# A mixture-of-experts loop: search and gather one rank further ahead, and the turning of a rank's inner layer inside the next rank's first product

## The chip, the cores and the metric

The kernel runs on one core of a Trainium2 chip. The metric is device time in microseconds (us) of one execution. Engines: TensorE (PE; its weight loads are PEld), VectorE (DVE), ScalarE (ACT), GpSimd (POOL), SyncE (SP), which issues loads, and the DMA engines.

## The reference, cut to what matters

One step of a decoder trunk for 520 tokens (512 of a prompt, 8 samples): a combined projection, a state-space branch, dilated attention, two layer norms, and a mixture of 64 experts of which each token takes 8. The change lies in the experts:

```python
for b in blocks:                                  # one expert and the tokens that chose it
    xb = x_pad[tok]                               # gather of its tokens' rows, 1024 wide
    h = jax.nn.silu(xb @ w1[e]) * (xb @ w3[e])    # inner layer, 256 wide
    yb = (h @ w2[e]).astype(jnp.float32)
    acc = acc.at[tok].add(yb * g[:, None])        # scatter, weighted by the gate
```

All in float32. Every expert's weights (w1, w3, w2) are read from HBM once.

## The kernel before

Each float32 operand is split into a high part (ScalarE, L269) and a low part (VectorE, L265; one weight chunk of each expert on GpSimd, L265 too), and a product is three matmuls: high x high, high x low, low x high.

The first 440 us are projection, attention, state space, routing. Then comes the loop over ranks: experts in order of how many tokens they have, most first. `CAPS[e]` (112 down to 56) is the number of rows held for rank e. For a rank e:

- `find(e)`: a small matmul (`x<-what,oh`) looks up the tokens of the rank; VectorE makes their numbers `idx` (L1396). `gather(e)` (L1414, GpSimd) has a DMA fetch their rows to `XG[e % 3]`, one of three buffers, so it waits until rank e-3's rows are turned. `fetch(e)` is both.
- `turn(e)`: eight TensorE transposes of `xg` (L215), in two halves with a PSUM bank each, split into `xgh` and `xgl`.
- `expert_in(e)`: the first product, four weight chunks q0 to q3 of 512 KB, six matmuls each (`a<-hi,xgh`, `a<-lo,xgh`, `a<-hi,xgl`). `ffn_mid` at its end makes `hg` on ScalarE and then VectorE (L259).
- `ffn_turn(e)`: two transposes of `hg` (`a<-ident,hg`), split into `hh` (ScalarE) and `hl` (VectorE). Here it is called H.
- `expert_out(e)`: the second product, chunks k0 and k1, twelve matmuls in six pairs (`mm<-hi,hh`, `mm<-lo,hh`, `mm<-hi,hl`, twice), then `y` (L1450) and a scatter that adds it in HBM (L1451, GpSimd).

Weight chunks are loaded by SyncE in one sequence (L318), in the order q0 to q3 of rank e, then k0 and k1 of rank e-1; raw buffers come free when a chunk is split. Between ranks stands further work of other layers (`x<-ph,x1h` and the like). The transposes of `xg` and `hg` and the first product share three PSUM banks (`bank()`, names `a`).

No order is written out by hand in the loop: a scheduler orders each engine's instructions from the program order, a simulated time line and the constraints given to it (`issue_after`). Each engine then carries out its list in order.

Of the kernel before, what the change touches and what calls it, by code (L numbers as in the profile page):

```python
# [11 lines left out]
def _quiet(*args, **kwargs):  # L12
# [19 lines left out]
NE = 64  # L32
FIXED = 2
CAPS = ([112] * 3 + [100] * 1 + [94] * 1 + [92] * 1 + [88] * 2 + [86] * 1 + [84] * 3 + [82] * 2 + [78] * 7 + [76] * 2 + [74] * 4
        + [72] * 5 + [70] * 4 + [68] * 4 + [66] * 5 + [64] * 7 + [62] * 3 + [60] * 2 + [58] * 2 + [56] * 5)
# [165 lines left out]
def trunk_step(ctx: ExitStack, tc: tile.TileContext, I, O):  # L201
# [3 lines left out]
    class Tensor:  # L205
# [3 lines left out]
        def matmul(self, *a, **k):  # L209
            ins = nc.tensor.matmul(*a, **k)  # L210
            if self.pinned:
                tc.keep_in_program_order(ins)

        def transpose(self, *a, **k):
            ins = nc.tensor.transpose(*a, **k)  # L215
            if self.pinned:
                tc.keep_in_program_order(ins)

    T = Tensor()
# [35 lines left out]
    def bank():  # L255
        return psa.tile([128, 512], F32, tag="a", name="a")
# [10 lines left out]
    def split(hi, lo, src, e=V):  # L267

        a = S.activation(hi, src, AF.Copy)  # L269
        return a, sub(e, lo, src, hi.bitcast(F32))  # L270
# [976 lines left out]
    def ffn_in(out, xth, xtl, hi, lo, q, rows):  # L1247

        for k in range(2):
            kk = 2 * q + k  # L1250
            for n, (l, w) in enumerate(((xth, hi), (xth, lo), (xtl, hi))):
                T.matmul(out, lhsT=l[:, kk, rows], rhs=w[:, k], start=(kk == 0 and n == 0), stop=(kk == 7 and n == 2))

    def ffn_mid(ps, m):
        hg = moe.tile([MAX_CAP, 256], F32, tag="hg", bufs=2, name="hg")
        S.activation(hg[0:m], ps[0:m, 0:256], AF.Silu)
        mul(V, hg[0:m], hg[0:m], ps[0:m, 256:512])
        return hg

    def ffn_turn(hg, m):  # L1260
        ps = bank()
        for k in range(2):
            T.transpose(ps[:, m * k:m * k + m], hg[0:m, 128 * k:128 * k + 128], ident[0:m, 0:m])
        hh, hl = (moe.tile([128, 2, MAX_CAP], F32R, tag=nm, bufs=2, name=nm)[:, :, 0:m] for nm in ("hh", "hl"))
        H['turned'] = split(hh, hl, ps[:, 0:2 * m].rearrange("p (k t) -> p k t", k=2))
        return hh, hl
# [9 lines left out]
    def shared_mid(out, hg):  # L1276
        S.activation(hg, out[:, 0:128], AF.Silu)
        mul(V, hg, hg, out[:, 128:256])
        return hg

    def shared_turn(hg, i, c):

        ps = bank()
        T.transpose(ps[:, 0:TT], hg, ident[0:TT, 0:TT])
        split(H['shared'][:, i, 0, c], H['shared'][:, i, 1, c], ps[:, 0:TT])
# [93 lines left out]
    XG, XT, HG, HT, GC, IX = {}, {}, {}, {}, {}, {}  # L1379
# [3 lines left out]
    def find(e, what=(0, 1)):  # L1383

        m = CAPS[e]
        if e not in OH:
            OH[e] = one_hot(e, m)
        a, b = what[0], what[-1] + 1
        ps = psx.tile([128, 512], F32, tag="x", name="x") if e > 2 else bank()
        for i in R5:  # L1390
            T.matmul(ps[0:m, 3 * a:3 * b], lhsT=OH[e][:, i], rhs=H['what'][:, i, 3 * a:3 * b, e], start=(i == 0), stop=(i == 4))
        both = moe.tile([128, 2], F32, tag="gc", bufs=8, name="both")
        V.tensor_reduce(both[0:m, a:b], ps[0:m, 3 * a:3 * b].rearrange("p (w n) -> p w n", n=3), axis=AX.X, op=ALU.add)
        if 0 in what:
            IX[e] = moe.tile([128, 1], I32, tag="idx", bufs=8, name="idx")
            H['last'] = V.tensor_scalar(IX[e][0:m], both[0:m, 0:1], 1024.0, H['slots'][0:m], op0=ALU.add, op1=ALU.min)  # L1396
        if 1 in what:
            GC[e] = both[:, 1:2]
            if e < NE - 2:
                OH.pop(e)  # L1400
# [7 lines left out]
    def fetch(e):  # L1408
        find(e)
        gather(e)  # L1410

    def gather(e):
        m = CAPS[e]
        G.indirect_dma_start(out=XG[e % 3][0:m], out_offset=None, in_=xD[:, :],  # L1414
                             in_offset=bass.IndirectOffsetOnAxis(ap=IX[e][0:m, 0:1], axis=0),
                             bounds_check=NT - 1, oob_is_err=False)

    def turn(e):
        x, m = XG[e % 3], CAPS[e]
        XT[e] = [moe.tile([128, 8, MAX_CAP], F32R, tag=nm, bufs=2, name=nm)[:, :, 0:m] for nm in ("xgh", "xgl")]  # L1420
        for z in range(2):
            ps = bank()
            for j in range(4):
                k = 4 * z + j
                T.transpose(ps[:, m * j:m * j + m], x[0:m, 128 * k:128 * k + 128], ident[0:m, 0:m])
            src = ps[:, 0:4 * m].rearrange("p (k t) -> p k t", k=4)
            split(XT[e][0][:, 4 * z:4 * z + 4], XT[e][1][:, 4 * z:4 * z + 4], src)

    def expert_in(e):
        ps, m = bank(), CAPS[e]  # L1430
        for q in range(4):
            hi, lo = (t.rearrange("p (k n) -> p k n", k=2) for t in stream.get(AT[e] + q))
            ffn_in(ps[0:m], *XT[e], hi, lo, q, slice(0, m))
        HG[e] = ffn_mid(ps, m)
        XT.pop(e)

# [40 lines left out]
    def second_phase():  # L1477
# [124 lines left out]
        for e in range(NE + 1):  # L1602
            if e == NE - 1:
                last_rows()
            if 0 < e < NE:
                expert_in(e)
            if 0 < e < NE - 1:
                turn(e + 1)
            if e:
                expert_out(e - 1)  # L1610
            else:
                H['shared'] = py.tile([128, 5, 2, 2, TT], F32R, tag="side", name="st")
                mids = py.tile([MAX_CAP, 1024], F32, tag="y", bufs=YB, name="mids")
                mids = [shared_mid(H['first half'][i], mids[0:TT, 128 * i:128 * i + 128]) for i in R5]
            if 0 < e < 6:
                shared_turn(mids[e - 1], e - 1, 0)
            if 0 < e < NE - 1:
                HT[e] = ffn_turn(HG.pop(e), CAPS[e])
            if e + 3 < NE:
                fetch(e + 3)  # L1620
            for i in {SECOND + 2: (0, 1, 2), SECOND + 3: (3, 4)}.get(e, ()):
                second_sums(i)
            if e == 4:
                close_pool(pre)
                pw = open_pool("pw")
            while side and (e - 4) * SIDE >= N_SIDE - len(side) + 1:
                q, i = side.pop(0)
                if q == -2:
                    shared_more(i)
                elif q == -1:  # L1630
                    shared_out(i)
                elif q < 4:
                    layer_inputs(q, i)
                else:
                    last_scales(i)
# [198 lines left out]
    close_pool(gpool)  # L1834
    close_pool(qkv)
    second_phase()


# [16 lines left out]
```

## Time and profile before

| | us |
|---|---|
| median of 3 runs (1320.13 to 1326.46) | 1321.36 |
| profiled execution | 1323.58 |
| its span | 1321.8 |
| TensorE busy | 1182.6 (89%) |
| VectorE busy | 933.0 (71%) |
| ScalarE busy | 702.9 (53%) |
| GpSimd busy | 459.2 (35%) |

HBM moved 234 GB/s over the span; the mean granted TensorE clock was 0.946. Busy times are of the whole span; matmuls overlap, so a busy TensorE needn't be at its peak. Where TensorE isn't the one that is waited for, another engine's idle time costs nothing.

### The profile page before, as it was taken

What the parts mean: (1) busy time and instruction counts of PE and PEld (TensorE: products, weight loads), DVE (VectorE), ACT (ScalarE), POOL (GpSimd) and SP (SyncE); (2) the same over time, 40 slices, a digit from 0 to 9 for tenths busy, and PEclk for the clock granted to TensorE, in tenths of its full rate; (3) what the DMA queues carried; (4) which work ended last, traced back from release to release, by engine and by line L of the source; (5) the groups of instructions that cost most, each with busy time, mean ns of one, the idle gap of its engine ahead of it and who ended that gap; (6) DMA issues with size and microseconds to landing.
All of it is one profiled execution on the core that took longest, in us unless ns stands there. A gap on an engine that the chain in (4) does not pass through costs nothing. (4 is left out here: it accounts for less than half of the span.)

```text
span 1321.8 us, 20417 instructions
## 1 busy us (share of the span) xinstructions
PE 1182.6 (89%) x7082; PEld 884.3 (67%) x7084; DVE 933.0 (71%) x1440; ACT 702.9 (53%) x1055; POOL 459.2 (35%) x285
## 2 busy tenths in 40 slices
PE   6899999999997969888799888899899999988783
PEld 6899899899876846566566566677666666644341
DVE  7965658643487768576779666787878887766566
ACT  3232434233213656566567556677757767666463
POOL 1000000000012346343555335454555455465326
PEclk8899799999998879889999889999999999999897
DMA  9446553252523789889989978999999999979973
GB/s 367 158 135 167 198 162 129 72 155 83 180 77 106 246 217 274 254 263 304 296 254 314 290 237 278 285 329 314 321 311 313 335 314 299 303 249 289 260 230 97
DMA packets 112315, 312.92 MB, mean 237 GB/s; under 512 B 35121, under 2 KB 35545, under 8 KB 111135
## 3 DMA queue, kind: packets, MB, share of 16 engines
q1 hardware_dynamic: 78408, 261.74, 58.8%
q0 software_dynamic: 30848, 43.33, 14.8%
q10 hardware_dynamic: 2953, 6.52, 1.8%
q8 instruction: 57, 0.93, 0.3%
q14 instruction: 49, 0.40, 0.1%
HBM read 276.32 MB, written 32.87 MB: 234 GB/s over the span
## 5 line engine op out<-in xcount | busy, mean ns | idle before, releaser
L265 DVE TENSOR_TENSOR lo<-raw,hi 128x1024 fp32r<-128x1024 f32 x371 | 503.2, 1367 | 203.4 <-ACT hi L269 202.2
L269 ACT ACTIVATE hi<-raw 128x1024 fp32r<-128x1024 f32 x434 | 450.8, 1056 | 279.3 <-DMA raw<-in_we_dram 115.8
L210 PE MATMUL a<-hi,xgh 128*64 128x512 f32 (+18 forms) x512 | 212.3, 415 | 8.5 <-ACT hi L269 6.2
L1451 POOL DMA_INDIRECT accD<-y,idx x62 | 123.2, 1988 | 277.8 <-ACT hh L269 155.6
L210 PE MATMUL a<-lo,xgh 128*64 128x512 f32 (+18 forms) x512 | 210.9, 412 | 6.6 <-DVE lo L265 6.3
L210 PE MATMUL a<-hi,xgl 128*64 128x512 f32 (+18 forms) x512 | 207.0, 404 | 0.0
L265 POOL TENSOR_TENSOR lo<-raw,hi 128x1024 fp32r<-128x1024 f32 x63 | 168.3, 2672 | 62.5 <-ACT hi L269 51.8
L1414 POOL DMA_INDIRECT xg<-xD,idx x64 | 119.0, 1859 | 120.8 <-DVE idx L1396 57.9
L210 PE MATMUL mm<-xh,hi 128*128 128x260 f32 (+2 forms) x576 | 121.3, 292 | 16.6 <-ACT xh L269 6.6
L210 PE MATMUL mm<-xh,lo 128*128 128x260 f32 (+1 forms) x576 | 120.1, 290 | 1.8 <-DVE lo L265 1.8
L210 PE MATMUL mm<-xl,hi 128*128 128x260 f32 (+1 forms) x576 | 120.7, 291 | 0.8 <-DVE xl L265 0.8
L210 PEld LDWEIGHTS a<-hi,xgh 128*64 128x64 f32 (+18 forms) x512 | 75.7, 148 | 53.1 <-ACT hi L269 10.2
L210 PEld LDWEIGHTS a<-lo,xgh 128*64 128x64 f32 (+18 forms) x512 | 75.7, 148 | 45.4 <-DVE lo L265 10.7
L210 PEld LDWEIGHTS mm<-xh,hi 128*128 128x128 f32 x576 | 92.1, 195 | 17.5 <-ACT xh L269 6.3
L210 PEld LDWEIGHTS a<-hi,xgl 128*64 128x64 f32 (+18 forms) x512 | 75.7, 148 | 38.5 <-issue 4.3
L210 PE MATMUL mm<-lo,hh 128*64 128x512 f32 (+18 forms) x256 | 85.5, 416 | 12.8 <-POOL lo L265 9.9
L210 PEld LDWEIGHTS mm<-xh,lo 128*128 128x128 f32 x576 | 92.3, 195 | 2.1 <-DVE lo L265 2.0
L210 PEld LDWEIGHTS mm<-xl,hi 128*128 128x128 f32 x576 | 92.3, 195 | 1.5 <-DVE xl L265 1.1
L210 PE MATMUL mm<-hi,hh 128*64 128x512 f32 (+18 forms) x256 | 85.7, 417 | 8.0 <-ACT hi L269 7.6
L1450 ACT ACTIVATE y<-mm,both 78x1024 f32<-78x1024 f32 (+19 forms) x62 | 68.6, 1106 | 32.9 <-PE mm L210 29.8
L269 ACT ACTIVATE xgh<-a 128x256 fp32r<-128x256 f32 (+17 forms) x128 | 51.0, 408 | 63.7 <-PE a L215 63.0
L215 PEld LDWEIGHTS a<-ident,xg 64*128 64x128 f32 (+18 forms) x512 | 51.1, 147 | 48.9 <-issue 20.0
(410 smaller groups left out, 1919.4 us busy)
## 6 DMA issues: line engine op xcount, KB each, us to landing
raw<-in_we_dram SPq DMA_DIRECT2D x384, 512.0 KB
raw<-in_wd_dram SPq DMA_DIRECT2D x50, 512.0 KB
accD<-zeros_b POOLq DMA_DIRECT2D x2, 2560.0 KB, 23.7
praw<-in_wp_dram SPq DMA_DIRECT2D x8, 512.0 KB
base<-in_xtok_dram ACTq DMA_DIRECT2D x1, 2080.0 KB
xD<-base SPq DMA_DIRECT2D x5, 416.0 KB
base<-accD POOLq DMA_DIRECT2D x5, 416.0 KB, 22.8
acc<-accD SPq DMA_DIRECT2D x5, 416.0 KB
```

Of the source, the lines that this page charges most:

```text
L210: ins = nc.tensor.matmul(*a, **k)
L215: ins = nc.tensor.transpose(*a, **k)
L265: return e.tensor_tensor(out=o, in0=a, in1=b, op=ALU.subtract)
L269: a = S.activation(hi, src, AF.Copy)
L1414: G.indirect_dma_start(out=XG[e % 3][0:m], out_offset=None, in_=xD[:, :], in_offset=bass.IndirectOffsetOnAxis(ap=IX[e][0:m, 0:1], axis=0), ...
L1450: S.activation(y.rearrange("p (h n) -> p h n", h=2), ps[0:m], AF.Copy, scale=GC.pop(e)[0:m])
L1451: G.indirect_dma_start(out=sumsD[e % 2 if e < SECOND else 0][:, :], out_offset=bass.IndirectOffsetOnAxis(ap=IX.pop(e)[0:m, 0:1], axis=0), ...
```

## The change

Two things move. `fetch(e+3)` at the end of an iteration becomes `fetch(e+4)` ahead of `expert_out(e-1)`. And H of rank e-1, which stood behind `expert_out` of the rank before it, is now made inside `expert_in(e)`, held behind the last matmul of its second chunk (`issue_after`). No operation is added or removed.

```diff
@@ -210,6 +210,7 @@
             ins = nc.tensor.matmul(*a, **k)
             if self.pinned:
                 tc.keep_in_program_order(ins)
+            return ins
 
         def transpose(self, *a, **k):
             ins = nc.tensor.transpose(*a, **k)
@@ -1249,7 +1250,8 @@
         for k in range(2):
             kk = 2 * q + k
             for n, (l, w) in enumerate(((xth, hi), (xth, lo), (xtl, hi))):
-                T.matmul(out, lhsT=l[:, kk, rows], rhs=w[:, k], start=(kk == 0 and n == 0), stop=(kk == 7 and n == 2))
+                ins = T.matmul(out, lhsT=l[:, kk, rows], rhs=w[:, k], start=(kk == 0 and n == 0), stop=(kk == 7 and n == 2))
+        return ins
 
     def ffn_mid(ps, m):
         hg = moe.tile([MAX_CAP, 256], F32, tag="hg", bufs=2, name="hg")
@@ -1430,7 +1432,10 @@
         ps, m = bank(), CAPS[e]
         for q in range(4):
             hi, lo = (t.rearrange("p (k n) -> p k n", k=2) for t in stream.get(AT[e] + q))
-            ffn_in(ps[0:m], *XT[e], hi, lo, q, slice(0, m))
+            ins = ffn_in(ps[0:m], *XT[e], hi, lo, q, slice(0, m))
+            if q == 1 and e > 1:
+                with tc.issue_after(ins.ins):
+                    HT[e - 1] = ffn_turn(HG.pop(e - 1), CAPS[e - 1])
         HG[e] = ffn_mid(ps, m)
         XT.pop(e)
 
@@ -1606,6 +1611,8 @@
                 expert_in(e)
             if 0 < e < NE - 1:
                 turn(e + 1)
+            if e and e + 4 < NE:
+                fetch(e + 4)
             if e:
                 expert_out(e - 1)
             else:
@@ -1614,10 +1621,9 @@
                 mids = [shared_mid(H['first half'][i], mids[0:TT, 128 * i:128 * i + 128]) for i in R5]
             if 0 < e < 6:
                 shared_turn(mids[e - 1], e - 1, 0)
-            if 0 < e < NE - 1:
-                HT[e] = ffn_turn(HG.pop(e), CAPS[e])
-            if e + 3 < NE:
-                fetch(e + 3)
+            if e == 0:
+                fetch(3)
+                fetch(4)
             for i in {SECOND + 2: (0, 1, 2), SECOND + 3: (3, 4)}.get(e, ()):
                 second_sums(i)
             if e == 4:
```

What the scheduler makes of it, at three places. GpSimd, around the gather of rank 15 (`xg0`, the first gather row in both pieces); a DMA from `xD` is a gather, one to `accD` a scatter. Before:

```order
L265 TENSOR_TENSOR lo_6134<-raw_5972,hi_6133 128x1024
L1414 DMA xg0_4199<-xD_146,idx_6224 78x1024
L1451 DMA accD1_148<-y_6204,idx_5644 640x1024
L265 TENSOR_TENSOR lo_6287<-raw_6125,hi_6286 128x1024
L1451 DMA accD0_147<-y_6357,idx_5797 640x1024
L265 TENSOR_TENSOR lo_6408<-raw_6278,hi_6407 128x1024
L1414 DMA xg1_4201<-xD_146,idx_6377 78x1024
L1414 DMA xg2_4203<-xD_146,idx_6498 78x1024
```

Now, from the same gather on:

```order
L1416 DMA xg0_4199<-xD_146,idx_6051 78x1024
L1456 DMA accD0_147<-y_6081,idx_5340 640x1024
L266 TENSOR_TENSOR lo_6149<-raw_5980,hi_6148 128x1024
L1416 DMA xg1_4201<-xD_146,idx_6204 78x1024
L1456 DMA accD1_148<-y_6234,idx_5471 640x1024
L266 TENSOR_TENSOR lo_6302<-raw_6133,hi_6301 128x1024
L1416 DMA xg2_4203<-xD_146,idx_6357 78x1024
L1456 DMA accD0_147<-y_6387,idx_5624 640x1024
L266 TENSOR_TENSOR lo_6423<-raw_6286,hi_6422 128x1024
```

The gather of rank 16 (`xg1`) stood behind the scatters of ranks 11 and 12; it now stands behind the scatter of rank 10, ahead of that of rank 11.

TensorE, ranks 5 to 7: `hg_5171` is rank 5's, `a_5244` rank 6's first product, `xg1` rank 7's rows, `mm_5315` rank 5's second product, `hg_5296` rank 6's. Before:

```order
L215 MATMUL a_5222<-ident_69,hg_5171 128x92 x2
L210 MATMUL x_5496<-ph_5365,x1l_3788 104x256
L210 MATMUL a_5244<-hi_5191,xgh_5174 88x512
...
L210 MATMUL a_5244<-hi_5257,xgl_5175 88x512
L215 MATMUL a_5301<-ident_69,xg1_4201 128x88 x4
L215 MATMUL a_5308<-ident_69,xg1_4201 128x88 x4
L210 MATMUL mm_5315<-hi_5269,hh_5225 92x512 x2
L210 MATMUL mm_5315<-lo_5270,hh_5225 92x512 x2
L210 MATMUL mm_5315<-hi_5269,hl_5226 92x512 x2
...
L215 MATMUL a_5343<-ident_69,hg_5296 128x88 x2
L210 MATMUL a_5375<-hi_5316,xgh_5299 88x512
```

Now `hg_5186` is rank 5's, `a_5252` rank 6's first product, `mm_5345` rank 5's second product:

```order
L210 MATMUL a_5252<-hi_5233,xgl_5190 88x512
L216 MATMUL a_5277<-ident_69,hg_5186 128x92 x2
L210 MATMUL a_5252<-hi_5253,xgh_5189 88x512
...
L216 MATMUL a_5316<-ident_69,xg1_4201 128x88 x4
...
L210 MATMUL mm_5345<-hi_5284,hh_5280 92x512 x2
L210 MATMUL mm_5345<-lo_5285,hh_5280 92x512 x2
L216 MATMUL a_5323<-ident_69,xg1_4201 128x88 x4
L210 MATMUL mm_5345<-hi_5284,hl_5281 92x512 x2
L210 MATMUL mm_5345<-hi_5296,hh_5280 92x512 x2
```

H of rank 5 moved from ahead of rank 6's first product to its middle, and H of rank 6 no longer stands between rank 5's second product and rank 7's first. The second half of rank 7's turn moved from ahead of rank 5's second product to between its second and third pair.

VectorE at the same ranks. Before: `lo_5258` is the last chunk of rank 6's first product, `lo_5282` the last of rank 5's second product, `lo_5317` and `lo_5329` the first two of rank 7.

```order
L265 TENSOR_TENSOR lo_5258<-raw_5124,hi_5257 128x1024
L265 TENSOR_TENSOR st_4601<-a_5218,st_4601 128x104
L265 TENSOR_TENSOR hl_5226<-a_5222,hh_5225 128x2x92
L265 TENSOR_TENSOR lo_5282<-raw_5148,hi_5281 128x1024
L265 TENSOR_TENSOR lo_5317<-raw_5163,hi_5316 128x1024
L265 TENSOR_TENSOR lo_5329<-raw_5195,hi_5328 128x1024
L259 TENSOR_TENSOR hg_5296<-hg_5296,a_5244 88x256
L265 TENSOR_TENSOR lo_5377<-raw_5207,hi_5376 128x1024
```

Now `lo_5266` is the last chunk of rank 6's first product, `lo_5297` the last of rank 5's second product, `lo_5347` and `lo_5359` the first two of rank 7:

```order
L266 TENSOR_TENSOR lo_5266<-raw_5132,hi_5265 128x1024
L266 TENSOR_TENSOR st_4601<-a_5248,st_4601 128x104
L266 TENSOR_TENSOR lo_5297<-raw_5163,hi_5296 128x1024
L266 TENSOR_TENSOR lo_5347<-raw_5178,hi_5346 128x1024
L266 TENSOR_TENSOR hl_5281<-a_5277,hh_5280 128x2x92
L266 TENSOR_TENSOR lo_5359<-raw_5225,hi_5358 128x1024
L260 TENSOR_TENSOR hg_5311<-hg_5311,a_5252 88x256
```

`hl` of rank 5 stood behind the last chunk of rank 6's first product; it now stands behind the first chunk of rank 7 as well.

## Rows read from the trace of the kernel before

**Rows 1.** Time by stage: busy PE, PEld, DVE, ACT, POOL, then clock, DMA share, GB/s.

```profile
440.00:883.00 443.00, 385.01 (x2065) 269.30 (x2064) 323.23 (x440) 277.25 (x386) 201.26 (x94) 0.93 0.88 273
883.00:1161.00 278.00, 270.65 (x1562) 179.13 (x1560) 225.53 (x308) 198.64 (x274) 139.17 (x68) 1.00 0.99 314
1161.00:1276.00 115.00, 93.98 (x412) 46.73 (x411) 68.13 (x87) 66.47 (x93) 55.08 (x29) 0.93 0.88 263
```

**Rows 2.** The waits, whole span: us in total, times, longest us.

```profile
ACT hi L269 <- DMA raw<-in_we_dram: 115.8, 83, 3.6
PE a L215 <- DVE hg L259: 23.7, 13, 4.1
PE a L215 <- DMA xg<-xD,idx: 21.5, 5, 10.5
SPq L318 <- DVE lo L265: 328.1, 166, 13.8
```

**Rows 3.** TensorE in order of time, at ranks 4, 16 and 56.

```profile
489.33 1.02 PE L215 MATMUL a<-ident,xg 94*128 94x94 f32 x5 [10.49 <-DMA xg<-xD,idx]
...
659.58 1.30 PE L215 MATMUL a<-ident,xg 78*128 78x78 f32 x8 [5.81 <-DMA xg<-xD,idx]
660.62 1.12 PE L210 MATMUL mm<-lo,hh 128*78 128x512 f32 x2
...
664.94 0.47 PE L215 MATMUL a<-ident,hg 78*128 78x78 f32 x2
...
1171.22 0.68 PE L215 MATMUL a<-ident,xg 60*128 60x60 f32 x4 [4.07 <-DMA xg<-xD,idx]
1171.83 1.11 PE L210 MATMUL mm<-hi,hh 128*62 128x512 f32 x2
```

**Rows 4.** GpSimd in order of time (L1414 gather, L1451 scatter); last row: gathers' landing.

```profile
615.71 1.04 POOL L1414 DMA_INDIRECT xg<-xD,idx  x1 [0.85 <-DVE idx L1396]
623.32 1.49 POOL L1451 DMA_INDIRECT accD<-y,idx  x1 [6.57 <-ACT sg L1277]
...
640.01 1.80 POOL L1414 DMA_INDIRECT xg<-xD,idx  x1 [0.20 <-issue]
...
1140.80 2.55 POOL L265 TENSOR_TENSOR lo<-raw,hi 128x1024 fp32r<-128x1024 f32 x1
...
1154.63 1.23 POOL L1414 DMA_INDIRECT xg<-xD,idx  x1 [0.30 <-issue]
...
DMA to landing us min/median/max: 6.7/13.1/24.4
```

**Rows 5.** TensorE, then VectorE, at the end of rank 5 and start of 7.

```profile
528.41 0.68 PE L210 MATMUL mm<-hi,hh 128*92 128x512 f32 x2
...
529.40 0.62 PE L210 MATMUL mm<-hi,hl 128*92 128x512 f32 x2
...
533.43 0.37 PE L215 MATMUL a<-ident,hg 88*128 88x88 f32 x2 [2.02 <-DVE hg L259]
535.79 0.50 PE L210 MATMUL a<-hi,xgh 128*88 128x512 f32 x1 [1.99 <-DVE xgl L265]
...
530.37 1.23 DVE L265 TENSOR_TENSOR lo<-raw,hi 128x1024 fp32r<-128x1024 f32 x1 [2.32 <-ACT hi L269]
...
532.97 0.41 DVE L259 TENSOR_TENSOR hg<-hg,a 88x256 f32<-88x256 f32 x1
...
535.22 0.95 DVE L265 TENSOR_TENSOR xgl<-a,xgh 128x352 fp32r<-128x352 f32 x2
```

**Rows 6.** VectorE, then TensorE, at ranks 1 and 55 each.

```profile
464.86 4.40 DVE L265 TENSOR_TENSOR lo<-raw,hi 128x1024 fp32r<-128x1024 f32 x2 [0.52 <-ACT hi L269]
...
467.81 0.70 PE L210 MATMUL mm<-hi,hh 128*112 128x512 f32 x2
...
1185.61 1.20 DVE L265 TENSOR_TENSOR lo<-raw,hi 128x1024 fp32r<-128x1024 f32 x1
...
1184.25 0.61 PE L210 MATMUL mm<-hi,hh 128*60 128x512 f32 x2
```

## Prediction

> **What bounds the kernel now.** I began with the time by stage [rows 1]. The expert loop runs from about 440 to 1276 us of a 1321.8 us span. From 440 to 883 us TensorE is busy 385.01 of 443.00 us at a granted clock of 0.93 and the DMA engines are at 0.88 of their share: neither is full. From 883 to 1161 us both are: 270.65 of 278.00 us at 1.00, and 0.99. From 1161 to 1276 us it is 93.98 of 115.00 us, 0.93 and 0.88. So a wait that is taken away can only pay outside the middle stage, and only as far as weights come sooner too.
>
> Then the waits [rows 2]. TensorE waits for `hg` (VectorE's product after the first matmuls of a rank) ahead of the turn of the inner layer, 13 times, 23.7 us in all, 4.1 at most; for a gather 5 times, 21.5 us. ScalarE, which makes the high part of every weight chunk, waits 83 times for the raw weights, 115.8 us, and SyncE's loads wait 166 times (328.1 us, over the whole span) until VectorE's low part has freed a buffer. These two close a loop: loads wait for splits, splits for loads. Whatever makes TensorE faster has to be fed out of that loop.
>
> Last the places. The three large gather stalls are ranks 4, 16 and 56 [rows 3]: 10.49, 5.81 and 4.07 us. After such a stall the matmuls run at the lower clock level for a while: rank 16's five pairs of the second product begin at 660.62 and end where 664.94 begins, 0.86 us a pair [rows 3], where two pairs beside a full clock take 0.99 from 528.41 to 529.40 [rows 5].
>
> **The change, first part: search and gather earlier.** It adds no work: the same 64 searches and gathers are issued, from another place. What matters is where the gather stands in GpSimd's own queue, behind a scatter and a low part or before them. Rank 16 (GpSimd's rows in the change section): its gather was issued at 640.01, behind the scatter of 623.32 and three instructions after it [rows 4], and the rows landed for the matmul at 659.58. In the new order it stands ahead of that scatter. Its buffer is free once rank 13's rows are turned, which was done before the gather of 615.71 [rows 4], so it can go at about 616 to 623: 17 to 24 us earlier than before, where 5.81 were missing. Rank 56: its gather of 1154.63 moves ahead of a scatter to behind the low part of 1140.80 (2.55 us) [rows 4], about 11 us earlier where 4.07 were missing. Both stalls should vanish. A gather takes 13.1 us to land at the median and up to 24.4 [rows 4], so an earlier issue of that size is worth more than the scatter among gathers.
>
> Rank 4 stays: its gather is the same row of GpSimd's list in both kernels; the matmul that waited for it began at 489.33 [rows 3]. A different neighbourhood could change this (rank 5's gather now stands right behind it), so I keep 0 for it, with a bound of 10.49.
>
> Sum of this part: idle 5.81 + 4.07 = 9.88; clock 5 x (0.86 - 0.495) = 1.8 at rank 16, and an estimate of 1.0 at rank 56 from a pair of 1.11 [rows 3] against 0.62 [rows 5]: together 12.7 us. How much of it stays? During a stall raw weights go on arriving until the buffers are full, and the matmuls behind it feed on them. Both places are in stages that are neither TensorE's nor DMA's entirely [rows 1]. With nothing that decides, I take half: -6.4, with bounds of 0 and -12.7.
>
> **Second part: the turn of the inner layer (H) moves from behind the second product of the rank before into the first product of the next rank,** 12 of its 24 matmuls in. TensorE no longer stands still for `hg` there, but it is not free then: the next matmuls need weights and their own turned rows. Ranks 5 and 6 show it [rows 5]. TensorE ends rank 5's second product near 531.4, waits 2.02 us for `hg` (done 533.38), turns, and then waits 1.99 us more for `xgl`, which began on VectorE at 535.22 behind another low part. With the turn moved the first wait disappears and the second one grows by as much: nothing is gained. Where only `hg` was late, it stood behind one low part of 1.23 us [rows 5], and about that much plus `hg`'s own 0.41 is won. If 3 of the 13 places win 1.6 us each, that is 4.9; I take -5, with bounds of 0 and -23.7 [rows 2].
>
> **Third part: what the new order couples.** VectorE carries out its list in order, and the part of the turned inner layer that it makes, `hl`, now stands elsewhere in it. Before, `hl` of rank e stood behind low parts of rank e+1's first product in 61 of 64 ranks, which TensorE needs anyway before it comes to rank e's second product. In the new order it is so in only 33; in 15 it stands behind the low part of the second product's own last chunk, in 16 behind the first chunk of rank e+2 (rank 5 in the change section). The third pair of the second product needs `hl`, and the second half of the next rows' turn takes the PSUM bank that `hl` frees. So in these ranks TensorE waits for a chunk that it wants only later. I priced it from the trace: the end of that low part against the start of the second product plus 0.99 for two pairs. For rank 5: the low part of 530.37 ends 531.60, and `hl` after it was wanted at 528.41 + 0.99 = 529.40 [rows 5]; 2.2 us late. Of ranks 0 to 60, 18 come out late, the first rank 1 by 0.5 (low parts from 464.86 lasting 4.40, product 467.81) and the last rank 55 by 1.6 (1185.61 + 1.20, product 1184.25) [rows 6], 34 us in all.
>
> These 34 us are not 34 us of time. The lateness of neighbours is one and the same lag: weights do not come later for it, and once TensorE runs 2 us behind them the next rank is not late. It also fills idle time that is there: rank 5's 2.2 us fall into the 4.0 us that TensorE then waited anyway [rows 5]. What stays is a small lag in each of the few stretches. I take +4, with bounds of 0 (all of it falls into old idle time) and +34 (all paid).
>
> **Sum.** The profiled execution took 1323.58 us, 2.2 above the median of 1321.36. 1323.6 - 6.4 - 5 + 4 = 1316.2; brought to the median, **1314.0 us**. A measurement of this kernel can tell about 0.5% (6.6 us) from no change, so faster means below 1314.8 and slower above 1328.0.
>
> **The rivals.**
>
> *Weights pace it.* Then TensorE's waits are moved, not removed: with the stalls gone TensorE meets the next chunk sooner and waits for it. For it speak the 0.99 of 883 to 1161 us and the 115.8 us of waits for raw weights [rows 1, 2]; against it the 0.88 in the other two stages, where the stalls are. All of -6.4 and -5 is handed back but 2: about 1319. The Trainium skill ("Perfetto Trace Analysis", Identifying the Most-Contended Engine) says to work on the most contended engine, with HBM utilisation as the measure for DMA; by it this rival would hold for the whole loop, and the trace agrees for the middle stage alone.
>
> *Slower: `hl` behind a later chunk.* If the lag isn't absorbed, because a TensorE that lags frees split buffers later, so that splits, and through them loads, come later too, then half of the 34 us is paid rank after rank, and H wins nothing: +17 - 6.4 = +10.6, about 1332. Slower than 1328.0 begins where some 13 us of the 34 are paid. For it speaks the loop of 328.1 us [rows 2]; against it that ranks 14 to 26 and most of the middle stage are not late.
>
> *More is won.* The gathers' gain stays whole (12.7), H brings 8, the coupling costs 2: -18.7, about 1303. For it speaks that loads wait for splits more than splits for loads [rows 2]. Should rank 4's stall vanish too, it would be up to 10.49 lower still.
>
> *The change doesn't do what it says.* From rank 20 to 39 every gather already stands ahead of the scatter five ranks below it in the old order too; if ranks 16 and 56 stalled for contention and not for their place, nothing is won: 1321 to 1325.
>
> **How the numbers follow.** My forecast (1306 to 1322) has 0.42, two thirds of it below 1314.8; weights pace it 0.19; slower by `hl` 0.22; more is won 0.11; no effect 0.06. Faster: 0.28 + 0.11 + 0.04 (of the weights' case) = 0.43. Slower: 0.22 and 0.03 from the last case's upper end, 0.25. Same: 0.32. The range goes down to 1299 (more is won, with part of rank 4) and up to 1335 (the slower rival at its price and a little more), leaving about 0.08 below and 0.11 above.
>
> **What will show it.** Right, if no wait for a gather stands at ranks 16 and 56 and their gathers are issued some 17 and 11 us earlier; if the row "PE a <- DVE hg" falls from 23.7 to a few us; and if new idle time inside the second product (released by `hl` or by a low part) stays below 10 us. Wrong on the first part, if waits for raw weights or for low parts grow by the 10 us that the gathers free. Wrong on the third, if TensorE's idle time at the third pair or at the turn's second half exceeds 13 us, or if the busy share of 883 to 1161 us falls. The rank 4 stall should still be there with about 10 us; were it gone, the time would be below my forecast for a reason that I left out.

## The result, and the profile after

The changed kernel takes 1333.67 us (median of 5 runs, 1332.94 to 1337.5) where the kernel before, on the same chip, takes 1324.39 (5 runs, 1320.13 to 1326.46): a ratio of 1.0082, interval 1.0053 to 1.0111. It is slower by some 9 to 11 us, where the forecast was 1314.0 against 1321.36, some 7 us faster. The profiled execution took 1332.94 us with a span of 1331.2.

The time by stage of the kernel after, columns as in [rows 1]:

```profile
440.00:883.00 443.00, 370.15 (x1984) 255.44 (x1983) 318.13 (x427) 273.31 (x374) 195.30 (x92) 0.95 0.87 266
883.00:1161.00 278.00, 271.35 (x1586) 181.75 (x1585) 223.46 (x307) 196.69 (x272) 136.74 (x69) 1.00 0.98 314
1161.00:1276.00 115.00, 97.04 (x428) 48.09 (x427) 74.28 (x89) 67.55 (x93) 54.19 (x29) 0.94 0.88 267
```

The loss is in the first of the three stages. There TensorE is busy 370.15 us and carries out 1984 matmuls, where before it was 385.01 us and 2065 [rows 1]. The middle stage is as full as before. DMA isn't fuller in the first stage either: 266 GB/s against 273.

The waits of the kernel after, over the whole span (us in total, times, longest us); first TensorE's, then ScalarE's:

```profile
PE mm L210 <- POOL lo L266: 15.6, 11, 3.3
PE a L216 <- DVE sg L260: 13.8, 5, 5.4
...
PE a L216 <- DVE hl L266: 10.3, 9, 2.9
PE mm L210 <- ACT hh L270: 9.2, 6, 3.3
PE a L216 <- DMA xg<-xD,idx: 8.3, 2, 7.0
...
ACT hi L270 <- DMA raw<-in_we_dram: 147.9, 98, 5.8
```

The two waits that the change was to remove are down. TensorE waits 8.3 us for gathers (21.5 before), and the row "PE a <- DVE hg" of 23.7 us [rows 2] has fallen to 0.7 and is gone from the turn of the inner layer, as the group of that line shows (the number behind the bar's second part is the idle time before it, and what ended it):

```profile
L216 PE MATMUL a<-ident,hg 64*128 64x64 f32 (+17 forms) x128 | 20.3, 239 | 3.7 <-DVE xgl L266 3.7
```

In their place stand a low part that GpSimd makes (15.6), `sg` (13.8), `hl` (10.3) and `hh` (9.2), and ScalarE waits 32 us longer for raw weights than in [rows 2]. `sg` is the inner layer of a further expert that every token goes through; it uses the same two buffers as `hg`. The kernel before has no row of TensorE for `hl`, and for the other three:

```profile
PE mm L210 <- POOL lo L265: 9.9, 11, 1.6
...
PE a L215 <- DVE sg L259: 3.2, 2, 1.8
...
PE mm L210 <- ACT hh L269: 0.4, 1, 0.4
```

TensorE at the three places of [rows 3] in the kernel after, ranks 4, 16 and 56 (start, duration, idle before in brackets), and then the gathers of ranks 16 and 56 on GpSimd, with two rows of rank 16's inputs, the `idx` that its search makes (VectorE) and the end of rank 13's turn (TensorE):

```profile
486.35 0.86 PE L216 MATMUL a<-ident,xg 94*128 94x94 f32 x4 [6.97 <-DMA xg<-xD,idx]
...
663.93 0.43 PE L216 MATMUL a<-ident,xg 78*128 78x78 f32 x4
...
1179.59 0.45 PE L216 MATMUL a<-ident,xg 60*128 60x60 f32 x4
```

```profile
629.94 1.22 POOL L1416 DMA_INDIRECT xg<-xD,idx  x1 [9.46 <-PE mm L210]
632.22 1.51 POOL L1456 DMA_INDIRECT accD<-y,idx  x1 [1.06 <-ACT y L1455]
...
1147.71 1.24 POOL L1416 DMA_INDIRECT xg<-xD,idx  x1 [6.55 <-PE a L216]
...
628.93 0.20 DVE L1398 TENSOR_SCALAR idx<-both,slots 78x1 int32<-78x1 f32 x1
...
628.43 0.45 PE L216 MATMUL a<-ident,xg 82*128 82x82 f32 x4
```

No stall is left at ranks 16 and 56. Their gathers are issued 10.07 and 6.92 us earlier by the clock than in [rows 4], ahead of the scatter, in a loop that runs later by then. That is less than the 17 and 11 us of the forecast. Note the brackets: each gather now stands 6 to 9 us at the head of GpSimd's queue before it can go, with the scatter behind it. Rank 16's `idx` is there at 628.93 + 0.20 = 629.13, and rank 13's rows are turned at 628.43 + 0.45 = 628.88, both within about 1 us of the gather's start at 629.94.

### The profile page after: what moved, and what is told of

It reads as the page before. It is cut to its first block, busy times and chain, and to the rows that moved or that the text cites. A ratio compares the mean times of both kernels' runs of the same rounds, so it can differ in the third digit from the quotient of the medians.

```text
span 1331.2 us, 20434 instructions
## 1 busy us (share of the span) xinstructions
PE 1179.3 (89%) x7083; PEld 878.5 (66%) x7084; DVE 940.5 (71%) x1440; ACT 705.9 (53%) x1055; POOL 455.2 (34%) x285
## 3 DMA queue, kind: packets, MB, share of 16 engines
q0 software_dynamic: 30848, 43.33, 14.8%
## 5 line engine op out<-in xcount | busy, mean ns | idle before, releaser
L266 DVE TENSOR_TENSOR lo<-raw,hi 128x1024 fp32r<-128x1024 f32 x371 | 516.4, 1402 | 219.9 <-ACT hi L270 215.8
L210 PE MATMUL a<-hi,xgh 128*64 128x512 f32 (+18 forms) x512 | 210.0, 410 | 20.7 <-ACT hi L270 12.7
L210 PE MATMUL a<-lo,xgh 128*64 128x512 f32 (+18 forms) x512 | 208.5, 407 | 11.9 <-DVE lo L266 11.7
L1456 POOL DMA_INDIRECT accD<-y,idx x62 | 129.5, 2089 | 206.7 <-ACT y L1455 116.4
L266 POOL TENSOR_TENSOR lo<-raw,hi 128x1024 fp32r<-128x1024 f32 x63 | 175.3, 2782 | 56.7 <-ACT hi L270 44.1
L1416 POOL DMA_INDIRECT xg<-xD,idx x64 | 107.4, 1678 | 213.5 <-PE a L216 63.4
L210 PE MATMUL mm<-lo,hh 128*64 128x512 f32 (+18 forms) x256 | 85.7, 417 | 16.3 <-POOL lo L266 15.6
L210 PE MATMUL mm<-hi,hl 128*64 128x512 f32 (+18 forms) x256 | 85.4, 416 | 0.0
```

The costliest lines, as they stand in the source:

```text
L266: return e.tensor_tensor(out=o, in0=a, in1=b, op=ALU.subtract)
L1456: G.indirect_dma_start(out=sumsD[e % 2 if e < SECOND else 0][:, :], out_offset=bass.IndirectOffsetOnAxis(ap=IX.pop(e)[0:m, 0:1], axis=0), ...
```

## The experiments

The ratios are against the kernel before, run on the same chip in the same round. Times of single executions of one kernel spread by some 0.5% to either side.

**The two parts, one at a time.** The first has only the hunks of `fetch`, the second only those of H, with `fetch(e + 3)` at the end of an iteration as before. The first:

```diff
+            if e and e + 4 < NE:
+                fetch(e + 4)
             if e:
                 expert_out(e - 1)
...
-            if e + 3 < NE:
-                fetch(e + 3)
+            if e == 0:
+                fetch(3)
+                fetch(4)
```

The second:

```diff
...
             ins = ffn_in(ps[0:m], *XT[e], hi, lo, q, slice(0, m))
+            if q == 1 and e > 1:
+                with tc.issue_after(ins.ins):
+                    HT[e - 1] = ffn_turn(HG.pop(e - 1), CAPS[e - 1])
...
-            if 0 < e < NE - 1:
-                HT[e] = ffn_turn(HG.pop(e), CAPS[e])
```

> The change's first part alone: search and gather stand one rank further ahead, H stays behind the second product. Theory A (the loss is TensorE waiting for hh and hl, which stand behind later weight chunks since H was moved): this kernel is not slower than before, about 1314 to 1322 us, with the gather waits at ranks 16 and 56 gone; hl stands behind in+1 chunks as before. Theory B (the loss is GpSimd's list: a gather that waits for its buffer stands ahead of a scatter, the scatter comes late and holds the y and idx buffers, and ScalarE and VectorE stand still for them): this kernel has the whole loss, about 1332 to 1336. Theory C (weights pace the loop whatever the order): 1320 to 1326.

> The change's second part alone: H stands inside the next rank's first product, search and gather stay at e+3 at the end of the iteration. Here hl stands behind the first chunk of rank e+2 in 15 ranks and behind the second product's last chunk in 13, nearly as in the changed kernel (16 and 15). Theory A: about 1331 to 1337, with waits for hl, hh and sg between 500 and 690 us. Theory B: about 1318 to 1326, since the scatters stand where they did. Theory C: 1320 to 1326.

The first part alone: 1336.79 us, ratio 1.0102 (1.0066 to 1.0138). H alone: 1324.4, ratio 1.0019 (0.9996 to 1.0043). The whole loss is in the part that was to bring 6.4 us, and none that can be told from nothing is in the part with the new coupling. TensorE's waits of the first part alone, and of H alone:

```profile
PE a L215 <- DVE hg L259: 31.0, 16, 5.6
PE mm L210 <- POOL lo L265: 23.6, 14, 4.6
PE a L215 <- DMA xg<-xD,idx: 15.5, 3, 7.6
```

```profile
PE a L216 <- DMA xg<-xD,idx: 22.0, 4, 9.5
...
PE mm L210 <- POOL lo L266: 14.6, 9, 3.6
PE a L216 <- DVE sg L260: 12.6, 5, 4.9
PE a L216 <- DVE hl L266: 8.5, 11, 1.8
```

With the first part alone the gather waits shrink by 6.0 us, but those for GpSimd's low part grow from 9.9 to 23.6, and those for `hg` from 23.7 to 31.0. With H alone the `hg` row falls to 0.7, and `sg` (12.6, from 3.2), `hl` (8.5) and more for the low part come instead. So the waits for `sg` and `hl` of the whole change come with H: the first part alone has 0.5 us for `sg` and none for `hl`. A caution: the profiled execution of the first part alone is the slowest of its six (1342.62), that of H alone the fastest of its twelve (1317.91).

**The coupling undone.** In the whole change the splits of the second product's weights are held behind `hh` and `hl`, so that `hl` doesn't come behind those chunks (first run, the diff); then in the same way also those of chunks q2 and q3 of the next rank (second run):

```diff
+        a, b = H['turned']
         for k in range(2):
-            hi, lo = stream.get(BT[e] + k)
+            with tc.issue_after(a.ins), tc.issue_after(b.ins):
+                hi, lo = stream.get(BT[e] + k)
```

> The changed kernel, with the splits of the next first product's chunks that the second product asks for held behind hh and hl of its own rank: hl then stands behind the second product's last chunk in 24 ranks and behind the first product's last in 40, and in none behind the first chunk of rank e+2. Theory A: about half of the loss is gone, 1325 to 1330. Theory B: 1332 to 1336 as the changed kernel.

> The changed kernel, with the splits of the second product's own chunks held behind hh and hl too: hl stands behind the first product's last chunk in 63 of 64 ranks. The coupling of H with later chunks is gone, everything else is as changed. Theory A: the whole loss is gone, 1312 to 1322. Theory B: 1332 to 1336 as the changed kernel. If holding the splits back costs more than it gives (a lagging TensorE then holds up VectorE), it is slower than the changed kernel, above 1338.

1337.09 us, ratio 1.012 (1.0078 to 1.0163), and 1359.96, ratio 1.029 (1.0253 to 1.0328). Taking `hl` out from behind the later chunks gains nothing in the first run, and in the second holding splits back costs far more than `hl` did. These runs alone can't part the gain from the cost of holding. But with the two before them, where the loss comes without H and H comes without a loss, Theory A falls.

**Distance or place.** First `fetch(e + 4)` where `fetch(e + 3)` stood, at the end; then `fetch(e + 3)` at the new place, ahead of `expert_out`. The second:

```diff
+            if e and e + 3 < NE:
+                fetch(e + 3)
             if e:
                 expert_out(e - 1)
...
-            if e + 3 < NE:
+            if e == 0:
                 fetch(e + 3)
```

> The unchanged kernel with the distance alone: search and gather for rank e+4, but still at the end of the iteration, behind the second product. Theory D (the distance costs: a rank more of searched and gathered tokens in flight): as e1, 1331 to 1340 us. Theory P (the place costs: the search ahead of the second product takes the PSUM bank and VectorE from it): 1318 to 1326. Theory O (any other order costs, since the old one is one of many and happens to be good): 1326 to 1340, with other stalls than e1.

> The unchanged kernel with the place alone: search and gather ahead of the second product, but for rank e+3. Theory D: 1318 to 1326 us. Theory P: 1331 to 1340. Theory O: 1326 to 1340.

Distance alone: 1326.81 us, ratio 1.0038 (1.0014 to 1.0062). Place alone: 1338.15, ratio 1.0109 (1.0068 to 1.015). It is mostly the place, though the distance by itself costs 0.4%, with an interval above nothing. Theory O, that any other order costs, isn't excluded: both runs lie in its 1326 to 1340, the first at the lower edge.

**Which ranks.** The first part in ranks 1 to 17 only, then from rank 18 on only. The first of these:

```diff
+            if 0 < e < 18:
+                fetch(e + 4)
             if e:
                 expert_out(e - 1)
...
-            if e + 3 < NE:
+            if e == 0:
+                fetch(3)
+                fetch(4)
+            if e > 18 and e + 3 < NE:
                 fetch(e + 3)
```

> e1's change in ranks 1 to 17 alone; from rank 19 on search and gather stand where they stood. Theory E (the loss arises between 500 and 690 us, where in e1 and in the changed kernel ScalarE waits 41 to 42 us for raw weights in place of 25, and what follows only carries it along): as e1, 1331 to 1340 us. If the loss is spread over the loop: about a third of it, 1324 to 1330.

> e1's change from rank 18 on alone. Theory E: no loss, and rank 56's gather stall is gone, 1314 to 1322 us. If the loss is spread over the loop: about two thirds of it, 1328 to 1336.

1337.91 us, ratio 1.0131 (1.0087 to 1.0175), and 1333.42, ratio 1.0095 (1.0059 to 1.013). Either half costs as much as the whole. So the cost isn't a sum of small costs per rank, and it isn't tied to the ranks of 500 to 690 us, though the early half alone suffices. Theory E, that the loss arises from 500 to 690 us, explains the first of these runs and not the second; a loss spread over the loop explains the second and not the first.

**Order or traffic.** If the moved gathers cost by what their DMAs do to scatters and weights, the cost must go when they move next to nothing. A bound in the gather does that without touching the order: the instructions of the two runs are those of the kernel before and of the first part alone, row for row, on every engine. From rank 5 on only token rows 0 and 1 are fetched, and the buffers keep old rows otherwise, so the outputs are no longer right. The gathers' packets stay, as the last section shows; what goes is their bytes.

```diff
-                             bounds_check=NT - 1, oob_is_err=False)
+                             bounds_check=NT - 1 if e < 5 else 1, oob_is_err=False)
```

> The kernel before, with the same instructions in the same order on every engine; from rank 5 on the gather's bound lets it fetch only token rows 0 and 1, so nearly all the movement of the gathers is left out (the rest of the three row buffers keeps old rows; outputs differ). It is the base for the run that follows. Both theories: somewhat faster than before, since 64 gathers' traffic and TensorE's waits for gathers (21.5 us) are gone: ratio 0.985 to 0.998.

> The first part alone (search and gather one rank further ahead, ahead of the second product), again with the rows 0 and 1 alone fetched from rank 5 on. Against the run of the kernel before with as little fetched: Theory M (it is the moved traffic of the gathers, landing beside scatters and weights, that costs) expects no difference, within 0.3%. Theory S (it is the order: the search's matmuls and VectorE's steps ahead of the second product, and what they move back) expects the whole loss still there, 0.8 to 1.2% above.

The base takes 1297.32 us (1294.11 to 1301.09), ratio 0.9807 (0.977 to 0.9843); with the first part it takes 1318.04 (1314.46 to 1320.24), ratio 0.9951 (0.993 to 0.9972). The second is 1318.04 / 1297.32 = 1.016 of the first. The loss is there in full, and a little more, without the gathers' bytes, so it comes from the order (or from what the packets alone do, which no run leaves out). TensorE's waits and ScalarE's for raw weights, in the base and then with the first part:

```profile
PE a L215 <- DMA xg<-xD,idx: 18.9, 4, 6.9
PE a L215 <- DVE hg L259: 15.6, 9, 4.0
PE mm L210 <- POOL lo L265: 13.3, 9, 2.8
...
ACT hi L269 <- DMA raw<-in_we_dram: 64.1, 39, 5.8
```

```profile
PE mm L210 <- POOL lo L265: 25.0, 13, 5.1
PE a L215 <- DVE hg L259: 23.2, 11, 5.7
PE a L215 <- DMA xg<-xD,idx: 6.1, 2, 5.3
...
ACT hi L269 <- DMA raw<-in_we_dram: 98.2, 52, 4.7
```

It is the same exchange as between the kernel before and the first part alone: the gather row falls by 12.8, GpSimd's low part grows by 11.7, `hg` by 7.6, and the waits for raw weights by 34.1, though no gather's data competes with them. The stage from 500 to 690 us, base and then first part (columns as in [rows 1]):

```profile
500.00:690.00 190.00, 162.98 (x851) 113.54 (x850) 136.59 (x186) 113.66 (x162) 92.41 (x41) 0.92 0.80 253
```

```profile
500.00:690.00 190.00, 153.82 (x777) 104.83 (x778) 125.48 (x166) 108.98 (x152) 81.36 (x38) 0.91 0.78 241
```

All engines and the DMA do less there, none more: these are waits, not an engine or a transfer that is full.

One chain of waits can be read off. GpSimd, ScalarE, VectorE and TensorE in the first part alone, around 640 us. The gather is rank 17's; the row of VectorE makes its `idx`, and the first of TensorE turns rank 14, whose buffer it takes:

```profile
639.60 2.00 POOL L1414 DMA_INDIRECT xg<-xD,idx  x1 [7.62 <-issue]
641.91 6.55 POOL L1451 DMA_INDIRECT accD<-y,idx  x1 [0.30 <-issue]
647.50 3.34 POOL L265 TENSOR_TENSOR lo<-raw,hi 128x1024 fp32r<-128x1024 f32 x1
...
637.64 1.11 ACT L1450 ACTIVATE y<-mm,both 82x1024 f32<-82x1024 f32 x1 [0.21 <-PE mm L210]
...
643.66 1.06 ACT L269 ACTIVATE hi<-raw 128x1024 fp32r<-128x1024 f32 x1 [0.31 <-PE a L210]
...
638.59 0.20 DVE L1396 TENSOR_SCALAR idx<-both,slots 78x1 int32<-78x1 f32 x1
...
634.33 0.70 PE L215 MATMUL a<-ident,xg 78*128 78x78 f32 x8
...
645.18 0.67 PE L210 MATMUL mm<-hi,hh 128*82 128x512 f32 x2
...
650.89 1.15 PE L210 MATMUL mm<-lo,hh 128*82 128x512 f32 x2 [4.63 <-POOL lo L265]
```

The gather waits 7.62 us at the head of GpSimd's queue. Its buffer has been free since 634.33 + 0.70 = 635.03; its `idx` comes at 638.59 + 0.20 = 638.79, and it goes 0.81 us later. So it waits for its own search and not for the buffer. The scatter behind it has its `y` at 637.64 + 1.11 = 638.75 and goes at 641.91, 3.2 us late: 0.85 of that is the gather's waiting, the rest the gather's own 2.00 us and the 0.30 behind it. The low part behind that has its high part by 643.66 + 1.06 = 644.72 at the latest (the product at 645.18 uses it) and starts at 647.50, at least 2.8 us late; it lasts 3.34 where one on VectorE takes 1.23 [rows 5]; and TensorE, which did the first pair at 645.18, stands until 650.89. The run without the gathers' data has the same chain, to a few hundredths:

```profile
629.99 2.00 POOL L1414 DMA_INDIRECT xg<-xD,idx  x1 [7.62 <-issue]
632.30 6.55 POOL L1451 DMA_INDIRECT accD<-y,idx  x1 [0.30 <-issue]
637.89 3.33 POOL L265 TENSOR_TENSOR lo<-raw,hi 128x1024 fp32r<-128x1024 f32 x1
...
641.28 1.15 PE L210 MATMUL mm<-lo,hh 128*82 128x512 f32 x2 [4.61 <-POOL lo L265]
```

A caution on the scatter's 6.55 us: the low part starts before it ends. The Trainium skill ("Perfetto Trace Analysis", GPSIMD Engine Instruction) calls a GpSimd instruction's span unreliable and advises the spacing of starts. The trace agrees that the spans don't add up: from start to start it is 5.59 us.

How much of the loss can this chain carry? The trace has every gather, `idx`, turn and scatter, so it can be added up. From rank 4 on, 38 gathers of the first part alone stand at the queue's head for 1 us or more: 26 of them go within 1 us of their `idx` (154.7 us of waiting), 12 within 0.31 us of the turn that frees their buffer (36.9 us). In the kernel before it is 17 (59.1 us) and 9 (24.4 us). So the gathers do wait 108 us more, and mostly for their search. But the scatters do not come later for it: from `y` to the scatter's start it is 48.4 us over all 62 of them, against 48.9 before (59.2 against 54.1 in the pair without data). And H alone, which costs nothing that can be told, has 136 us of such waits of gathers. The chain at 640 us is real, but waiting gathers that hold up scatters, Theory B, can't be where 13 us went.

**Which order.** Theory Q says that it is the gather's place in GpSimd's queue, Theory S that it is the search's place on TensorE and VectorE. Three ways were tried to tell them apart. First, the first part alone with each gather held behind the scatter (`SC`, set in the lines left out) of the product ahead of which it stood, the search left early (the diff); then the gather alone at the early place, with `find(e + 5)` at the end of the iteration and `gather(e + 4)` ahead of the product:

```diff
-                fetch(e + 4)
+                find(e + 4)
             if e:
                 expert_out(e - 1)
+                if e + 4 < NE:
+                    with tc.issue_after(SC[e - 1].ins):
+                        gather(e + 4)
...
```

> The first part alone, but the gather is held behind the scatter of the second product ahead of which it stood; the search stays where the first part has it, ahead of the second product. So GpSimd's order of gather directly ahead of scatter (55 times) becomes scatter directly ahead of gather (48 times). Theory M (the gather's place in the traffic costs): part of the loss goes, ratio 1.000 to 1.006. Theory S (the search's place costs): the loss stays, 1.009 to 1.013.

> The gather alone at the early place: gather(e+4) stands ahead of the second product as in the first part, but its search stands at the end of the iteration before, where searches stood in the kernel before. GpSimd's order is that of the first part (gather directly ahead of scatter 56 times). Theory Q (the gather's place in GpSimd's queue costs: it waits there for its row buffer, with a scatter and a low part behind it): the loss stays, ratio 1.008 to 1.013. Theory S (the search's place on TensorE and VectorE costs): the loss falls to that of a longer distance alone, 1.002 to 1.005.

1330.33 us, ratio 1.0049 (1.0025 to 1.0073): half of the loss is gone with the gather behind the scatter, and what is left can't be told from the distance's own 1.0038. The search is still early there, so Theory S, which expects 1.009 to 1.013, falls as the whole account. 1352.16 us, ratio 1.0229 (1.0195 to 1.0264): with the gather alone early, the loss is twice as large, outside what either theory expects. This run doesn't decide between them, since its waits aren't those of the first part. Its gathers wait for their buffer (27 waits of 1 us or more, 115.0 us) rather than for `idx` (7, 21.5 us). GpSimd's low part is at 12.0 us there, and `xgl` has a row that the first part has at 2.6:

```profile
PE a L210 <- DVE xgl L265: 22.0, 5, 14.3
PE mm L210 <- POOL lo L265: 12.0, 9, 2.4
```

Second, the low part that GpSimd makes given to VectorE, in the kernel before and with the first part:

```diff
-                split(hi, lo, raw, G if 0 < m < 6 * (NE - 1) and m % 6 == 2 else V)
+                split(hi, lo, raw)
```

> The kernel before with the low part of the chunk that GpSimd splits given to VectorE, so that nothing but gathers and scatters is in GpSimd's queue in the loop. Base for the next run. Both theories: slower than before, since VectorE gets 63 low parts of some 1.2 us more: 1.01 to 1.04.

> The first part alone, with all low parts on VectorE as in the run above. Against that run: Theory Q (a low part stuck behind the waiting gather on GpSimd costs) expects no loss left, within 0.3%. Theory S (search's place) expects 0.7 to 1.3% more time, as without this edit.

1373.43 us, ratio 1.0373 (1.0334 to 1.0411), and 1345.21, ratio 1.0171 (1.0138 to 1.0203). The first part now gains 2.1% (1345.21 / 1373.43). That no loss is left is the sign that Theory Q wants, but a gain of that size is outside its 0.3%, and the base is no fair one: its gathers came late in the new order, and TensorE waited for them 92.6 us.

```profile
PE a L215 <- DMA xg<-xD,idx: 92.6, 15, 13.2
```

Third, the gather's wait at the queue's head taken away by a fourth row buffer, its memory taken from the raw weights:

```diff
-RAW2 = 7
+RAW2 = 6
...
-        G.indirect_dma_start(out=XG[e % 3][0:m], out_offset=None, in_=xD[:, :],
+        G.indirect_dma_start(out=XG[e % 4][0:m], out_offset=None, in_=xD[:, :],
...
```

> The kernel before with four row buffers for the gathers instead of three, the memory taken from the raw weights (6 buffers instead of 7). Base for the two runs that follow. A gather still follows its search at the end of an iteration. Both theories: 0 to 1.5% slower than before, for the missing raw buffer.

> The first part alone, with four row buffers and 6 raw buffers as in the run above: the gather of rank e+4 needs the buffer of rank e, whose rows are long turned, instead of that of rank e+1, whose rows are just being turned. Against that run: Theory Q (the gather waits for its row buffer at the head of GpSimd's queue, with a scatter and a low part behind it) expects the loss gone, within 0.3%, or a gain up to 0.6%. Theory R (any other effect of the place, the buffer's wait has no part in it) expects 0.8 to 1.3% more time, as with three buffers.

> The whole change, with four row buffers and 6 raw buffers. Against the run of the kernel before with the same buffers: Theory Q expects 0.994 to 1.002. Theory R expects 1.006 to 1.011. If Q holds and the missing raw buffer is cheap, this kernel could be the fastest of all.

> The first part alone with 6 raw buffers instead of 7 and three row buffers: the control of the four-buffer pair, which differs from the run of the first part with four row buffers in the row buffers alone (1.0312 against the kernel before). Theory Q (the wait for the row buffer at the head of GpSimd's queue costs, the fourth buffer took that cost away): 1.038 to 1.046. Theory K (with one raw buffer less the raw weights pace everything, so that no cost of the first part can show there): 1.028 to 1.035.

The kernel before with these buffers: 1373.5 us, ratio 1.0371 (1.0336 to 1.0407), where 0 to 1.5% was expected. The first part: 1368.02, 1.0312 (1.0279 to 1.0344). The whole change: 1374.41, 1.0366 (1.0331 to 1.0402). The first part with 6 raw buffers and three row buffers: 1356.46, 1.0277 (1.0245 to 1.031). Against their own base the first part and the whole change cost nothing. But the control says that this isn't the fourth buffer's doing: with three it is as fast or faster, near what Theory K expects (1.028 to 1.035). The fourth buffer did take away waits for the buffer: 6 gathers stand 1 us or more for it, 17.7 us in all, against 22 and 55.3 us with three. The time didn't fall with them. That a raw buffer less hides the cost of the first part is argued: the kernel before with 6 raw buffers and three row buffers wasn't run. Theory Q in its narrow form, that it is the wait for the row buffer that costs, isn't borne out; with seven raw buffers that wait is the lesser part, 36.9 of 191.6 us.

## Why the prediction was wrong, point by point

**The step that failed** is the first part of the sum: "With nothing that decides, I take half: -6.4, with bounds of 0 and -12.7". The stalls went as it said, at both places. But the bounds left out a loss, and the part measured 1.0102, about +13 us. The step looked at what an earlier gather gives to the rank that waits for it, and put at nothing what the new place of search and gather does to the rest of the order. It also had the time of issue wrong. "So it can go at about 616 to 623" looks at the row buffer alone; the gather needs its search's `idx` too, and in the changed kernel neither was there before 628.88.

**What took the place of the stalls** is shown twice, with and without the gathers' bytes: GpSimd's low part, +13.7 and +11.7 us of TensorE's waiting, and `hg`, +7.3 and +7.6, against 6.0 and 12.8 won. Waits for raw weights grow as well. This is where TensorE stands, not why. In the whole change the low part's row grows by 5.7 us only, and `sg`, `hh` and `hl` carry the rest. With the gather behind the scatter the low part's row is still 23.1, though half of the loss is gone; with the first part in ranks 1 to 17 alone it is 15.5, though the loss is whole. So no one row measures the loss.

**What stays open** is the cause. The order of the first part costs some 1% with seven raw buffers; the bytes of its gathers and H don't, and the distance by itself costs 0.4%. The best lead is the gather's place ahead of the scatter, since moving it back takes half of the loss. How that place costs isn't shown; that a waiting gather holds up the scatter is not it, by the sums above. Each edit lets the scheduler move many other instructions, and kernels that differ in a few lines came out between 0.4% and 3.7% slower. A kernel whose order is that of the kernel before but for one queue wasn't made.

**H and the coupling.** The prediction had -5 and +4, together -1. H alone measured 1.0019 (0.9996 to 1.0043), between -0.5 and +5.7 us of 1324. The mechanisms were as described: the `hg` waits all but vanish, and `hl` is waited for, 8.5 us with H alone and 10.3 in the whole change, near the 10 us named as right and below the 13 named as wrong. The `sg` waits, +9.4 us with H alone, were not in the sum. That -5 and +4 came out near nothing is partly luck. The rival "slower by `hl`" gave about the measured time (1332), for a reason that isn't the right one: undoing the coupling brought 1.012, not a gain. That the measured time still lies below the 1335 of the range, whose upper end came from this rival, is luck.

**The rivals.** "Weights pace it" isn't what happened: the first stage's DMA does less, not the same. That waits for raw weights would grow if the first part were wrong was named as the sign, and they did, by 32 us. The gathers' bytes don't explain the grown waits: in the pair without them the waits grow by 34. Whether they follow the delays or cause part of them isn't shown.

**Rank 4** was kept at its 10.49 us [rows 3]. It has 6.97 now, so its neighbours do count for something, though little.

## What to carry to other kernels

Before you move a DMA issue ahead in an engine's queue, list everything that it waits for: here an issue that was to go 17 us earlier went 10 earlier, because what it needs, its search's result and its buffer, came late too. Price a moved instruction with a loss among the bounds, even where the stall that it removes is plain in the trace: the stalls went, and the kernel got slower. A chain that can be followed at one place isn't yet the cause: add it up over all places, as here, where the gathers waited 108 us more and the scatters behind them came no later. And where a scheduler makes the order, test a suspected transfer by leaving out its data and not its instruction: the order stays the same row for row, and bytes and order can be told apart.

## What the runs showed of the hardware that was not expected

Bounding the gathers to two token rows from rank 5 on took nearly all of their data away, but not their packets, and not GpSimd's time. The software DMA queue of the kernel before and of the same kernel with the bound (packets, MB, share of 16 engines), and then GpSimd's gathers in both (busy us, mean ns):

```profile
q0 software_dynamic: 30848, 43.33, 14.8%
...
L1414 POOL DMA_INDIRECT xg<-xD,idx x64 | 119.0, 1859 | 120.8 <-DVE idx L1396 57.9 <-PE a L215 27.7 <-DVE oh L1404 8.3
```

```profile
q0 software_dynamic: 30848, 28.00, 11.5%
...
L1414 POOL DMA_INDIRECT xg<-xD,idx x64 | 118.5, 1852 | 116.0 <-DVE idx L1396 59.9 <-PE a L215 26.3 <-DVE oh L1404 8.6
```

15.33 MB less moves in the same 30848 packets. A gather costs GpSimd 1.86 us with its rows and 1.85 without. The kernel takes 26.6 us less for it (1323.9 against 1297.32), where 15.33 MB at the 273 GB/s of the first stage [rows 1] would be 56 us of moving by itself. TensorE still waits 18.9 us for gathers (21.5 before). Of these, 7.05 are at ranks 3 and 4, which fetch all their rows; at ranks 16 and 56, whose gathers bring two rows at most, it waits 6.95 and 4.92 us, where it was 5.81 and 4.07 [rows 3]:

```profile
655.23 1.04 PE L215 MATMUL a<-ident,xg 78*128 78x78 f32 x6 [6.95 <-DMA xg<-xD,idx]
...
1147.80 0.68 PE L215 MATMUL a<-ident,xg 60*128 60x60 f32 x4 [4.92 <-DMA xg<-xD,idx]
```

As far as this pair tells, that wait is for the time from issue to landing more than for the amount that lands.
